# A decoder trunk in split fp32: the streamed activations take another place modulo 256 bytes, and stationary weight chunks are written 64 bytes further on

## The chip, the core and the metric

The kernel runs on one core of one Trainium2 chip. The metric is the device time of one execution in microseconds, and what is compared is the median of several runs. [...]

## What is computed

Two layers over 256 tokens of width 2048. Each layer is a mixing half and a feed-forward half, with a norm before and after each. Cut to what matters here:

```python
for l in range(DEPTH):                                  # DEPTH = 2
    hn = rms_norm(x, norm_mix_pre[l])
    proj = hn @ w_in[l]                                 # 2048 x 5888
    p_rwkv, p_attn, p_gmlp = jnp.split(proj, [...], axis=-1)
    y = concat(rwkv7_mix(p_rwkv), dilated_attention(p_attn), chunked_sgu(p_gmlp))
    x = x + rms_norm(y @ w_out[l], norm_mix_post[l])    # 2048 x 2048
    hn = rms_norm(x, norm_ffn_pre[l])
    up = hn @ ffn_up[l]                                 # 2048 x 11264
    conv = conv_b + causal_conv(up, width=3)
    gate, val = jnp.split(conv, 2, axis=-1)
    x = x + rms_norm((gelu(gate) * val) @ ffn_down[l], norm_ffn_post[l])   # 5632 x 2048
```

## The kernel before

Every large product is made in split form. A number is kept as a high part in fp32r, which TensorE takes as it is, and a low part, the rest. A product is then hi*hi + lo*hi + hi*lo, each of them a matmul in fp32r.

**Weights.** All large weights come through one stream of chunks, 128 partitions by 1024 numbers. SyncE's queue fetches a chunk into a tile raw (line 85), ScalarE casts it into whi (line 104), VectorE subtracts to make wlo (line 113). There are four buffers of whi and of wlo and three of raw (NB, RB = 4, 3). A few chunks at the seam between two halves go into other tiles instead (xw; xhi and xlo), for which extra holds a function. The list chunks names source and length of each chunk in the order of use; step() and wave_chunks() fill it.

**Activations.** act_tile() makes 16 tiles act of 512 numbers: 256 tokens of the high part, then 256 of the low part.

**Which operand is stationary.** TensorE holds one operand, 128 by 128, loaded by a weight load (PEld), and streams the other past it. The load for the next matmul runs while the present one streams.

- ws_step() (lines 528 and 529) holds the weights. For each of 16 blocks of the depth it streams all 512 numbers of act past whi, then the first 256 past wlo. It is used for the RWKV columns of w_in (output ps_r) and for ffn_up (ps_up).
- as_steps() (lines 554 to 556) holds the activations and streams the weights, 512 columns at a time (256 in one span and in a tail): high part past whi, high part past wlo, low part past whi. With act it is used for the other columns of w_in and for w_out; with hh and hl, the gated products of the feed-forward half, for ffn_down.
- Wave.part() (lines 315 to 318) is ws_step in 256 columns, for the first two outputs at the seam of two halves.

**Order.** Steps run in the order of the list steps, one chunk after another, and side work (the RWKV pairs, attention, the conv) is put between chunks by slot(), one piece of each generator at a time. The order of the instructions is thus that of the Python program; nothing is moved by a scheduler.

**Places.** The byte at which a tile starts in its partition follows from the order of allocation. In the built programs:

```text
tile                    start before  mod 256     start after  mod 256
act (16)                30976, ...       0        31200, ...     224
raw (3)                 184288, ...    224        182240, ...    224
whi, wlo (4 each)       196576, ...    224        194528, ...    224 (tile)
  written, stationary                  224                        32
  written, streamed                    224                       224
hh, hl (2 each)         94176, ...     224        94176, ...     224
xhi, xlo (3 each)       147424, ...    224        147424, ...    224
xw                                      32                         0
```

All blocks of 128 by 128 within these tiles begin a multiple of 512 bytes after the tile, so a block has the place of its tile.

Of the kernel before, what the change touches and what calls it, by code (L numbers as in the profile page):

```python
# [10 lines left out]
F32 = mybir.dt.float32  # L11
F32R = mybir.dt.float32r
# [8 lines left out]
P = 128  # L21
# [34 lines left out]
def tile_trunk(ctx, tc, x_d, xt_d, pos_d, cst_d, lvl_d, pcol_d, pcv_d, prow_d,  # L56
# [6 lines left out]
    const = ctx.enter_context(tc.tile_pool(name="const", bufs=1))  # L63
    wp = ctx.enter_context(tc.tile_pool(name="wp", bufs=NB, side="right"))
# [9 lines left out]
    chunks = []  # L74
# [5 lines left out]
    def emit_dma(upto=1 << 30):  # L80
        while st["dma"] < min(len(chunks), st["lo"] + RB, upto):
            w = st["dma"]
            src, n = chunks[w]
            raws[w] = wp.tile([P, 1024], F32, name="raw", bufs=RB)
            nc.sync.dma_start(raws[w][:, :n], src)
            st["dma"] += 1

    def emit_hi():
        w = st["hi"]
        if w == len(chunks):  # L90
            return
        if w in extra:
            pair = extra[w]()
            if pair is None:
                return
            hi, lo = pair
        elif sum(v not in extra for v in range(st["done"], w)) < NB:
            hi = wp.tile([P, 1024], F32R, name="whi")
            lo = wp.tile([P, 1024], F32R, name="wlo")
        else:  # L100
            return
        emit_dma()
        n = chunks[w][1]
        A.copy(hi[:, :n], raws[w][:, :n])  # L104
        whl[w] = (hi, lo)
        st["hi"] += 1

    def emit_lo():
        w = st["lo"]
        if w < st["hi"]:  # L110
            n = chunks[w][1]
            hi, lo = whl[w]
            V.tensor_tensor(lo[:, :n], raws.pop(w)[:, :n], f(hi[:, :n]), op=ALU.subtract)  # L113
            st["lo"] += 1
            emit_dma()

    def weight(ahead=0):
        while st["lo"] <= st["done"] + ahead:
            emit_hi()
            emit_lo()  # L120
        return whl[st["done"] + ahead]

    def mid():
        emit_hi()
        slot()

    def weight_done():
        del whl[st["done"]]
        st["done"] += 1
        emit_lo()  # L130
# [4 lines left out]
    def slot():  # L135
        for g in list(live):
            try:
                next(g)
            except StopIteration:
                live.remove(g)  # L140

    def boost():
        emit_hi()
        emit_lo()
# [2 lines left out]
        while live:  # L147
            slot()

    def step(srcs, fn):  # L150

        chunks.extend(srcs)
        steps.append(fn)


# [72 lines left out]
    def sumsq(src, acc, n, junk=None):  # L228
# [2 lines left out]
            junk = pmx.tile([P, 512], F32, name="junk", tag="mx")[:, :n]  # L231
        A.activation(junk, src, AF.Square, accum_out=acc)

    both = {}

    def act_tile():
# [20 lines left out]
    def big(n, name):  # L257
        return sm.tile([P, 2, ACOLS], F32, name=name, tag="big", bufs=1)[:, :, :n]
# [65 lines left out]
    def wave_chunks(tiles, post_in):  # L324
        if hasattr(post_in, "room"):
            for q in post_in.rooms:
                extra[len(chunks) + q] = lambda q=q: post_in.room(q)
        chunks.extend((t[0][:, h * 1024:(h + 1) * 1024], 1024) for h in range(2) for t in tiles)

    def rows_of(ss, wait=4, pool=None):  # L330

# [24 lines left out]
    def opening(gain0, act, tiles):  # L356
# [6 lines left out]
        q = xt.rearrange("p (c k) t -> p c (k t)", c=4)  # L363
        load(0)
        emit_dma(1)
        emit_dma(2)
        load(1)
# [150 lines left out]
    def ws_step(src, act, out, after):  # L518

        def fn():  # L520
            ps = out()
            for h in range(2):
                hi, lo = weight()
                for k in range(8):
                    kt = h * 8 + k
                    c = slice(k * P, (k + 1) * P)
                    ah, al = act[kt]
                    T.matmul(ps, hi[:, c], both[id(ah)][0], start=kt == 0, stop=False)  # L528
                    T.matmul(ps[:, S:], lo[:, c], ah, start=False, stop=kt == 15)  # L529
                    if k == 3:  # L530
                        mid()
                weight_done()
                if h == 0:
                    slot()
            after(ps)
            slot()
        step([(src[:, h * 1024:(h + 1) * 1024], 1024) for h in range(2)], fn)


    def as_steps(src, off, act, k0, nk, n, after, tail=0, more=False, late=0, hold=False):  # L540
# [67 lines left out]
    def add(items):  # L608
        for srcs, fn in items:
            step(srcs, fn)  # L610


    def mixing(l, post_in):
# [92 lines left out]
        def rw_tile(t, out, done=None):  # L706
            src, alloc, after = rw(t, out, done)
            ws_step(src, act, alloc, after)
# [516 lines left out]

        first = [rw(0, lambda: env["wa"], lora_w, pmx), rw(1, lambda: env["glo"], lora_g, pmx)]
        wave_chunks(first, post_in)
        steps.append(start)
        spans = [(0, 512), (512, 512), (1024, 512), (1536, 512), (2048, 256), (2304, 512), (2816, 512)]
# [84 lines left out]
        def evac1(n):  # L1314
            def after(i, ps):
                A.copy(env["yacc"][:, i, n * 512:(n + 1) * 512], ps)
            return after

        step([], pre1)
        step([], pre1b)  # L1320
        for n in range(4):
# [71 lines left out]
    def ffn(l, post_in):  # L1393
# [13 lines left out]
        def start():  # L1407
            boundary(l, "nffn", act, post_in(), first)
            fp = env["fp"] = es.enter_context(tc.tile_pool(name=f"fp{l}", bufs=1))
            env["pcv"] = fp.tile([P, NCV], F32, name="pcv")  # L1410
            nc.gpsimd.dma_start(env["pcv"], pcv_d[l])
            env["grow"] = fp.tile([P, D], F32, name="growf")
            nc.gpsimd.dma_start(env["grow"], bass.AP(tensor=prow_d.tensor,
                                                     offset=prow_d.offset + l * NPR + PR["nfp"],
                                                     ap=[[0, P], [1, D]]))
            fp.tile([P, 144], F32, name="gapf")
            env["yacc"] = big(D, "yaccf")
            env["ssq"] = sm.tile([P, 2, 5], F32, name="ssq", bufs=1)
            env["spare"] = lambda: fp.tile([P, 512], F32, name="yl", tag="pu", bufs=2)
# [53 lines left out]
        def up(g):  # L1473
            for q in range(1 if g == 0 else 0, GRP):
                for src, alloc, after in unit(g * GRP + q):
                    ws_step(src, act, alloc, after)
# [6 lines left out]

        first = [(wup[l, 0], alloc0, lambda ps: None), (wup[l, 1], alloc0, lambda ps: spawn(conv(0, pss)))]
        wave_chunks(first, post_in)
        steps.append(start)

        def down(g):
# [149 lines left out]
```

## Time and profile before

| | |
|---|---|
| median of 3 runs | 2491.04 us (2489.84 to 2491.28) |
| profiled execution | 2492.22 us |
| its span, first to last instruction | 2490.5 us |
| TensorE, matmuls | 98% of the span |
| VectorE, ScalarE, GpSimd | 71%, 54%, 22% |
| granted TensorE clock | 0.993 |
| DMA | 171 GB/s |

How to read it: the busy share of TensorE counts each matmul from its start to a modelled end, and matmuls overlap, so 98% does not say that it works at its peak. The rate is seen in the timeline of that engine, as the distance from one matmul's start to the next one's. [...]

The span runs through these stretches: 0 to 506 us the first layer's mixing half (RWKV pairs to 284), to 531 a seam, to 1248 its feed-forward half (up and down loops in turn), to 1267 a seam, to 1743 the second mixing half (RWKV pairs to 1520), to 1763 a seam, to the end the second feed-forward half.

### The profile page before, as it was taken

The page shows a single profiled execution, that of the slowest core. Times are in us where ns is not written, and L with a number is a line of the kernel's source. Part 1 is how long each engine was busy: PE and PEld are TensorE (multiplying, and loading weights), DVE is VectorE, ACT ScalarE, POOL GpSimd, SP SyncE. Part 2 cuts the span into 40 slices and gives each one's busy share as a digit, 9 for nine tenths or more (in the row PEclk, how much of TensorE's full clock was granted, in tenths as well). Part 3 has the DMA queues.
Part 4 walks back from the last instruction along what each step waited for, and adds up shares of the span by engine and source line. Part 5 has one row for each costly group of instructions (what it writes and reads, how often), then busy time and mean ns, then how long its engine had stood idle before and what let it go on. Part 6 is the DMA issues. An engine that isn't in the chain of part 4 may idle for free.

```text
span 2490.5 us, 37105 instructions
## 1 busy us (share of the span) xinstructions
PE 2432.9 (98%) x14010; PEld 2067.4 (83%) x14010; DVE 1760.1 (71%) x2584; ACT 1339.6 (54%) x2208; POOL 541.5 (22%) x512
## 2 busy tenths in 40 slices
PE   8999999999999999999999999999999999999998
PEld 7787787788888888888887877878888888888887
DVE  7889866577775675675678898665877756757755
ACT  5554545466555554554465555555665545545533
POOL 4224413031211120110232244132212101201102
PEclk9999999999999999999999999999999999999999
DMA  6343434645555555555543334345555565555554
GB/s 209 133 152 108 131 121 145 200 166 203 188 191 189 195 189 186 199 184 193 201 147 128 124 112 142 103 161 194 180 196 194 185 196 190 187 190 195 186 194 162
DMA packets 119762, 426.33 MB, mean 171 GB/s; under 512 B 13478, under 2 KB 13542, under 8 KB 119070
## 3 DMA queue, kind: packets, MB, share of 16 engines
q1 hardware_dynamic: 115776, 411.09, 49.0%
q0 software_dynamic: 2128, 9.59, 1.2%
q10 hardware_dynamic: 1678, 3.27, 0.5%
q8 instruction: 110, 1.80, 0.3%
q14 instruction: 70, 0.57, 0.1%
HBM read 421.80 MB, written 2.10 MB: 170 GB/s over the span
## 4 chain that ended last, share of the span: by engine, by line
PE 78%; DVE 7%; issue 6%; POOL 4%; ACT 3%; DMA 2%; DVEq 0%; POOLq 0%; ACTq 0%
PE ps_up L528 24%; PE ps_up L529 13%; PE ps_as L554 11%; PE ps_as L555 10%; PE ps_as L556 10%; PE ps_r L528 3%; DVE wlo L113 2%; PE ps_r L529 1%; DVE spl L821 1%; ACT whi L104 1%; POOL zv L1200 1%; DMA pcv<-in_pcv_dram 1%; POOL x L295 0%; DMA gws<-in_gws_dram 0%; ACT spl L830 0%
## 5 line engine op out<-in xcount | busy, mean ns | idle before, releaser
L113 DVE TENSOR_TENSOR wlo<-raw,whi 128x1024 fp32r<-128x1024 f32 (+1 forms) x785 | 975.4, 1250 | 385.6 <-ACT whi L104 383.7
L104 ACT CAST whi<-raw 128x1024 fp32r<-128x1024 f32 (+1 forms) x785 | 808.6, 1033 | 405.8 <-PE ps_as L556 168.7
L528 PE MATMUL ps_up<-act,whi 128*128 128x512 f32 x2752 | 954.7, 390 | 0.0
L529 PE MATMUL ps_up<-act,wlo 128*128 128x256 f32 x2752 | 776.2, 282 | 0.4 <-DVE wlo L113 0.3
L528 PEld LDWEIGHTS ps_up<-act,whi 128*128 128x128 f32 x2752 | 516.5, 188 | 108.1
L529 PEld LDWEIGHTS ps_up<-act,wlo 128*128 128x128 f32 x2752 | 520.1, 189 | 1.1 <-DVE wlo L113 1.0
L554 PE MATMUL ps_as<-whi,act 128*128 128x512 f32 (+1 forms) x712 | 289.5, 407 | 0.4 <-ACT act L253 0.4
L1457 POOL TENSOR_TENSOR cv<-cv,cv 128x256 f32<-128x256 f32 x88 | 70.6, 802 | 958.1 <-DVE cv L1452 958.1
L554 PE MATMUL ps_as<-whi,hh 128*128 128x512 f32 (+1 forms) x726 | 277.9, 383 | 0.0
L555 PE MATMUL ps_as<-wlo,hh 128*128 128x512 f32 (+1 forms) x726 | 277.8, 383 | 0.0
L556 PE MATMUL ps_as<-whi,hl 128*128 128x512 f32 (+1 forms) x726 | 277.7, 383 | 0.0
L556 PE MATMUL ps_as<-whi,act 128*128 128x512 f32 (+1 forms) x712 | 273.1, 384 | 0.0
L555 PE MATMUL ps_as<-wlo,act 128*128 128x512 f32 (+1 forms) x712 | 272.8, 383 | 0.0
L528 PE MATMUL ps_r<-act,whi 128*128 128x512 f32 x576 | 217.7, 412 | 0.0
L1435 ACT COPY pu<-ps_up 128x256 f32<-128x256 f32 x172 | 64.0, 372 | 255.8 <-PE ps_up L529 255.8
L529 PE MATMUL ps_r<-act,wlo 128*128 128x256 f32 x576 | 162.8, 283 | 0.0
L554 PEld LDWEIGHTS ps_as<-whi,hh 128*128 128x128 f32 x726 | 136.4, 188 | 26.9 <-DVE yaccf L1353 0.2
L556 PEld LDWEIGHTS ps_as<-whi,hl 128*128 128x128 f32 x726 | 136.4, 188 | 26.7
L555 PEld LDWEIGHTS ps_as<-wlo,hh 128*128 128x128 f32 x726 | 136.4, 188 | 26.5
L556 PEld LDWEIGHTS ps_as<-whi,act 128*128 128x128 f32 x712 | 134.1, 188 | 28.9 <-DVE act L254 0.4
L554 PEld LDWEIGHTS ps_as<-whi,act 128*128 128x128 f32 x712 | 134.7, 189 | 26.4 <-issue 4.0
L555 PEld LDWEIGHTS ps_as<-wlo,act 128*128 128x128 f32 x712 | 134.8, 189 | 21.9 <-DVE wlo L113 0.5
(380 smaller groups left out, 2950.2 us busy)
## 6 DMA issues: line engine op xcount, KB each, us to landing
raw<-in_wup_dram SPq DMA_DIRECT2D x352, 512.0 KB, 3.9
raw<-in_wdn_dram SPq DMA_DIRECT2D x160, 512.0 KB, 3.5
raw<-in_win_t_dram SPq DMA_DIRECT2D x104, 512.0 KB, 3.4
raw<-in_win_r_dram SPq DMA_DIRECT2D x80, 512.0 KB, 3.6
raw<-in_wo_dram SPq DMA_DIRECT2D x64, 512.0 KB, 3.6
raw<-in_wdn_dram SPq DMA_DIRECT2D x32, 256.0 KB, 2.7
xt<-in_xt_dram SPq DMA_DIRECT2D x4, 512.0 KB, 7.5
x<-in_x_dram ACTq DMA_DIRECT2D x4, 512.0 KB, 4.0
```

Of the source, the lines that this page charges most:

```text
L104: A.copy(hi[:, :n], raws[w][:, :n])
L113: V.tensor_tensor(lo[:, :n], raws.pop(w)[:, :n], f(hi[:, :n]), op=ALU.subtract)
L528: T.matmul(ps, hi[:, c], both[id(ah)][0], start=kt == 0, stop=False)
L529: T.matmul(ps[:, S:], lo[:, c], ah, start=False, stop=kt == 15)
L554: T.matmul(ps, ah[:, t], hi[:, c], start=kt == 0, stop=False)
L555: T.matmul(ps, ah[:, t], lo[:, c], start=False, stop=False)
L556: T.matmul(ps, al[:, t], hi[:, c], start=False, stop=kt == nk - 1)
L821: V.tensor_tensor(Sp[hs[1 - h], h], src[hs[h]], f(Sp[hs[h], h]), op=ALU.subtract)
L1200: G.tensor_tensor(vv[:, i], vv[:, i], rb_(nm), op=op)
L1435: A.copy(p[:, e], ps[e][:, S:])
L1457: G.tensor_tensor(cv[1], cv[0], cv[1], op=ALU.mult)
```

## The change

A gap of 224 bytes is allocated ahead of the act tiles, so that they start at place 224 modulo 256, as the weight tiles do. Another gap, in the feed-forward half, is made 224 bytes shorter, so that hh and hl stay where they were. Chunks get a third entry, whether they are held as the stationary operand; if so (ws_step and the waves), whi and wlo are written 16 numbers, 64 bytes, into their tile. The tiles grow from 1024 to 1088 numbers, 256 bytes, so that each of them starts at place 224 as before. Each engine carries out the same instructions in the same order on the same shapes; only addresses differ.

```diff
-            src, n = chunks[w]
+            src, n, _ = chunks[w]
...
-            hi = wp.tile([P, 1024], F32R, name="whi")
-            lo = wp.tile([P, 1024], F32R, name="wlo")
+            o = 16 * chunks[w][2]
+            hi, lo = (wp.tile([P, 1088], F32R, name=q)[:, o:o + 1024] for q in ("whi", "wlo"))
...
-    def step(srcs, fn):
-
-        chunks.extend(srcs)
+    def step(srcs, fn, still=False):
+
+        chunks.extend((*s, still) for s in srcs)
...
+    const.tile([P, 56], F32, name="gap")
     both = {}
 
     def act_tile():
...
-        chunks.extend((t[0][:, h * 1024:(h + 1) * 1024], 1024) for h in range(2) for t in tiles)
+        chunks.extend((t[0][:, h * 1024:(h + 1) * 1024], 1024, True) for h in range(2) for t in tiles)
...
-        step([(src[:, h * 1024:(h + 1) * 1024], 1024) for h in range(2)], fn)
+        step([(src[:, h * 1024:(h + 1) * 1024], 1024) for h in range(2)], fn, True)
...
-            fp.tile([P, 144], F32, name="gapf")
+            fp.tile([P, 88], F32, name="gapf")
```

## Rows read from the trace of the kernel before

**Rows 1.** The page: busy us and share by engine; clock in 40 slices.

```profile
PE 2432.9 (98%) x14010; PEld 2067.4 (83%) x14010; DVE 1760.1 (71%) x2584; ACT 1339.6 (54%) x2208; POOL 541.5 (22%) x512
...
PEclk9999999999999999999999999999999999999999
```

**Rows 2.** TensorE's waits: who waited for whom, us in total, times, longest.

```profile
PE ps_q L908 <- DVE X L919: 9.2, 12, 2.0
PE ps_t L437 <- DVE x L292: 6.9, 5, 3.0
PE ps_gm L1207 <- POOL zv L1200: 5.7, 2, 3.1
```

**Rows 3.** TensorE's timeline, as loop over act: start, us; first and last of 173.

```profile
439.70 0.40 PE L555 MATMUL ps_as<-wlo,act 128*128 128x512 f32 x1
...
479.83 0.40 PE L556 MATMUL ps_as<-whi,act 128*128 128x512 f32 x1
```

**Rows 4.** The same view, down loop over hh and hl: first and last of 178.

```profile
949.81 0.39 PE L556 MATMUL ps_as<-whi,hl 128*128 128x512 f32 x1
...
989.93 0.39 PE L556 MATMUL ps_as<-whi,hl 128*128 128x512 f32 x1
```

**Rows 5.** Instructions on single lines: ns min/median/max, first and last start.

```profile
L556 PE MATMUL ps_as<-whi,hl x726: 279/389/393, 764.5 to 2480.8; 128*128 128x512 f32 x171, 128*128 128x256 f32 x11
...
L556 PE MATMUL ps_as<-whi,act x712: 274/396/628, 48.8 to 1743.4; 128*128 128x512 f32 x158, 128*128 128x256 f32 x20
```

**Rows 6.** Windows of 46 us: TensorE busy (matmuls), clock, DMA share, GB/s; act, then hh.

```profile
435.00:481.00 46.00, 46.00 (x198) 1.00 0.60 195
...
950.00:996.00 46.00, 46.00 (x204) 1.00 0.58 191
```

**Rows 7.** Timeline of the up loop, weights stationary: first and last of 175.

```profile
2061.65 0.39 PE L528 MATMUL ps_up<-act,whi 128*128 128x512 f32 x1
2061.88 0.28 PE L529 MATMUL ps_up<-act,wlo 128*128 128x256 f32 x1
...
2091.81 0.39 PE L528 MATMUL ps_up<-act,whi 128*128 128x512 f32 x1
```

**Rows 8.** Timeline of the opening wave: eight matmuls of 256 columns, and the next.

```profile
21.22 1.09 PE L318 MATMUL ps_r<-act,whi 128*128 128x256 f32 x8
22.15 0.28 PE L315 MATMUL ps_r<-act,whi 128*128 128x256 f32 x1
```

**Rows 9.** TensorE's groups with shapes apart: count | busy us, mean ns | idle before.

```profile
L528 PE MATMUL ps_up<-act,whi 128*128 128x512 f32 x2752 | 954.7, 390 | 0.0
L529 PE MATMUL ps_up<-act,wlo 128*128 128x256 f32 x2752 | 776.2, 282 | 0.4 <-DVE wlo L113 0.3
L554 PE MATMUL ps_as<-whi,act 128*128 128x512 f32 x632 | 265.6, 420 | 0.4 <-ACT act L253 0.4
...
L528 PE MATMUL ps_r<-act,whi 128*128 128x512 f32 x576 | 217.7, 412 | 0.0
...
L555 PE MATMUL ps_as<-wlo,act 128*128 128x256 f32 x80 | 22.5, 281 | 0.0
L556 PE MATMUL ps_as<-whi,act 128*128 128x256 f32 x80 | 22.4, 280 | 0.0
```

**Rows 10.** Waits within 47:284 and 284:506; then windows: busy PE, PEld, DVE, ACT, POOL.

```profile
PE ps_q L908 <- DVE X L919: 5.2, 7, 1.9
...
PE ps_gm L1207 <- POOL zv L1200: 2.6, 1, 2.6
...
47.00:284.00 237.00, 226.44 (x1589) 184.93 (x1589) 204.25 (x392) 125.30 (x240) 74.25 (x78) 1.00 0.40 131
...
531.00:1248.00 717.00, 716.94 (x3840) 622.27 (x3839) 480.88 (x607) 390.24 (x564) 111.12 (x99) 1.00 0.57 194
```

**Rows 11.** The chunks' subtraction and cast into each kind of tile: ns min/median/max.

```profile
L113 DVE TENSOR_TENSOR wlo<-raw,whi x785: 682/1225/2605, 8.1 to 2471.0; 128x1024 fp32r<-128x1024 f32 x189, 128x512 fp32r<-128x512 f32 x8
...
L113 DVE TENSOR_TENSOR xw<-raw,xw x4: 1207/1210/1212, 506.0 to 1751.9; 128x1024 fp32r<-128x1024 f32 x4
...
L104 ACT CAST whi<-raw x785: 615/1052/1081, 7.0 to 2469.9; 128x1024 fp32r<-128x1024 f32 x189, 128x512 fp32r<-128x512 f32 x8
...
L104 ACT CAST xw<-raw x4: 1028/1042/1054, 502.9 to 1742.3; 128x1024 fp32r<-128x1024 f32 x4
```

**Rows 12.** Timeline of the second seam's wave, chunks of two places: first and last of 24.

```profile
527.09 0.28 PE L318 MATMUL ps_up<-act,whi 128*128 128x256 f32 x1
527.20 0.28 PE L318 MATMUL ps_up<-act,xw 128*128 128x256 f32 x1
...
529.80 0.28 PE L318 MATMUL ps_up<-act,xw 128*128 128x256 f32 x1
```

## What I expect, before the run

> **What bounds the kernel now.** I read the page's busy shares first: TensorE is busy 98% of the span, VectorE 71%, ScalarE 54%, at a granted clock of nine tenths or more in all 40 slices [rows 1]. Then the waits: the idle time ahead of TensorE, in 23 entries, comes to some 45 us in the whole span, the longest entry 9.2 us [rows 2]. So the end is set by how closely TensorE's matmuls follow one another, and the next view is the timeline of one engine, where the distance from start to start shows that.
>
> Three loops make nearly all of TensorE's time. The up loop (and the r loop of the mixing) has the weight chunk stationary and streams act, 512 columns for hi and 256 for lo. The two "as" loops stream the weights, 512 columns, past a stationary tile: act in the mixing, hh and hl in the down projection. The as loops issue the same instruction on the same shapes, from L554 to L556, yet differ. With act stationary, 172 intervals take from 439.70 to 479.83, which is 40.13 / 172 = 233.3 ns each; with hh and hl, 177 take from 949.81 to 989.93, which is 226.7 ns [rows 3, 4]. The durations agree: 396 against 389 ns, with no queue in between [rows 5]. In windows of the same 46 us 198 matmuls stand against 204, at the same granted clock of 1.00 and nearly the same DMA rate [rows 6].
>
> What else differs? The place of the operands in their partition, by the table of places ahead. I write d for the place modulo 256 of the tile whose weights are being loaded, less the place of the tile that streams meanwhile. With hh it is 224 - 224 = 0; with act it is 0 - 224, or +32. In the up and r loops it is 224 - 0, or -32. There a pair (512 and then 256 columns) takes from 2061.65 to 2091.81 for 87 pairs: 346.7 ns [rows 7].
>
> [...]
>
> **The change, part by part.**
>
> First, act moves from place 0 to place 224. For the as loops over act d becomes 0, as it is for hh. Of their matmuls 632 on each of the three lines have 512 columns [rows 9], so 1,896 intervals go from 233.3 to 226.7: 1,896 x 6.6 = 12.5 us less. The 240 with 256 columns I leave alone: at 280 to 281 ns on L555 and L556 they are no longer than the 282 ns of L529. Some of the gain is given back. In the as loops of the mixing other work runs between the chunks, and TensorE waits there 5.2 us for DVE X in the first pairs (seven waits) and 2.6 us for POOL zv [rows 10]; those chains keep their length while the matmuls that cover them get 3% shorter. I take 1.5 us for that, an estimate of about a tenth, and 11 us remain.
>
> Second, stationary weight chunks start 64 bytes on, at place 32, under act at 224: d in the up and r loops goes from -32 to +64. There are 2,752 + 576 = 3,328 pairs [rows 9], so each nanosecond of a pair is 3.3 us. No matmul of these loops has d = +64 in this trace, so I bound it by the nearest rows. [...] I take zero, and keep both ends for the range.
>
> Third, the chunks' cast and subtraction (L104, L113) write at place 32 from raw at 224, 64 bytes off, where both were at 224. The trace has just that pair of places: the xw tiles, at 32. Their cast takes 1042 ns against 1052 in the median, their subtraction 1210 against 1225 [rows 11]. This costs nothing.
>
> Fourth, the waves: 384 matmuls of 256 columns, whose loads go from -32 to +64, or to 0 for chunks in the tiles xhi and xlo, or stay at +32 (xw). At 4 ns each they are 1.5 us to either side, taken as zero. The rest is moved whole: tiles behind act go on by 224 bytes, hh and hl stay where they were because the second gap is 224 bytes shorter, and the ring of chunks grows downward into free space. No instruction is added, dropped or reordered, no DMA changes its size.
>
> The sum against the profiled execution, whose own time is 2492.2 us (span 2490.5 and 1.7 around it): 2492.2 - 11 = 2481 us. That execution lies 1.2 us over the median of the three runs, so against 2491.04 it is **2480 us**.
>
> [...]
>
> **The rivals.**
>
> The dear pair, which ends on the other side. At d = +64 a weight load meets the stream as it does at +32, since that is its nearest neighbour by address. It decides from a pair that is 11 / 3.3 = 3.3 ns dearer: there the two effects cancel. At 4.8 ns dearer the kernel is over 0.2% slower. [...] For it: the price is seen to rise from d = 0 to d = +32. Against it: in the mixed run of 256-column matmuls at +32 and -32, 23 intervals from 527.09 to 529.80 take 117.8 ns [rows 12], so +32 is not dear at every length.
>
> [...]
>
> Places are not the cause. The down loops run beside other work than the loops over act, and it may be that work, not the place, that makes 6.6 ns; reads of the stream and of the weights then don't meet at all. Then nothing moves: 2491 us. [...] Against it: clock and DMA rate are the same in the windows compared, and the excess is there in every interval.
>
> That the change doesn't do what it says is out: the built program has act at 224, the stationary chunks at 32, the streaming ones and hh at 224.
>
> **How the numbers follow.** The forecast, a pair within 1.6 ns of today's, lies between 2475 and 2486: chance 0.40. The cheap pair, below that: 0.26. The dear pair: from 1.6 to 4.8 ns it ends within 0.2% of before, 0.16; above that it is slower, 0.13. Places not the cause: 0.05, no change. Some 0.2%, or 5 us, is about what a measurement of this kernel can tell from no change. So faster 0.66, same 0.21, slower 0.13. The range goes from 2460 to 2497: it leaves out the last third of the cheap pair (about 0.07) and the upper part of the dear one (about 0.12).
>
> **What the profile after would show.** The as loops over act at 226.7 ns from start to start, 389 ns long, 204 matmuls in 46 us: the first term. [...] Down loops and the casts unchanged. If act's loops stay at 233, places are not the cause and the prediction is wrong at its root; if the pair moves by more than 2 ns, its second term is.

## The result: slower by 0.63%

The changed kernel takes 2508.15 us in the median of 6 runs (2504.57 to 2510.08), the kernel before 2492.38 (2489.84 to 2494.14, 6 runs). The ratio is 1.0063, with a 95% interval from 1.0053 to 1.0074. The forecast was 2480 us, and the range ended at 2497.

The profiled execution after the change has a span of 2508.4 us, 17.9 more than before. The granted clock is 0.992 of full speed, where it was 0.993. The page's first row, against [rows 1]:

```profile
PE 2446.5 (98%) x14010; PEld 2068.1 (82%) x14010; DVE 1762.0 (70%) x2584; ACT 1335.8 (53%) x2208; POOL 543.6 (22%) x512
```

TensorE's groups with shapes apart (lines behind the new gap are one higher: the loops are L529, L530 and L555 to L557); they answer to [rows 9]:

```profile
L529 PE MATMUL ps_up<-act,whi 128*128 128x512 f32 x2752 | 972.8, 397 | 0.0
L530 PE MATMUL ps_up<-act,wlo 128*128 128x256 f32 x2752 | 773.3, 281 | 0.0
...
L557 PE MATMUL ps_as<-whi,act 128*128 128x512 f32 x632 | 248.9, 394 | 0.0
L556 PE MATMUL ps_as<-wlo,act 128*128 128x512 f32 x632 | 247.7, 392 | 0.4 <-DVE wlo L113 0.4
```

The 512-column matmuls of the up loop last 397 ns where they lasted 390. Of the as loops over act, the second and the third matmul of a group last 392 and 394 ns; before they lasted 396 and 397:

```profile
L556 PE MATMUL ps_as<-whi,act 128*128 128x512 f32 x632 | 250.7, 397 | 0.0
L555 PE MATMUL ps_as<-wlo,act 128*128 128x512 f32 x632 | 250.3, 396 | 0.0
```

The windows of the two feed-forward halves tell where the time went (TensorE busy and matmuls first; the row of before is in [rows 10]):

```profile
530.00:1256.00 726.00, 726.00 (x3843) 622.03 (x3842) 480.22 (x607) 388.12 (x565) 113.01 (x99) 1.00 0.57 192
...
1772.00:2508.40 736.40, 726.93 (x3848) 622.72 (x3846) 485.10 (x614) 387.36 (x566) 116.36 (x101) 1.00 0.55 188
```

Each half takes 9 us more than before (726 against 717, 736.4 against 727.5). The timeline of TensorE in the second layer's up loop, first and last of 171 rows, as in [rows 7]:

```profile
2079.82 0.40 PE L529 MATMUL ps_up<-act,whi 128*128 128x512 f32 x1
2080.05 0.28 PE L530 MATMUL ps_up<-act,wlo 128*128 128x256 f32 x1
...
2109.85 0.40 PE L529 MATMUL ps_up<-act,whi 128*128 128x512 f32 x1
```

From 2079.82 to 2109.85 there are 85 pairs: 353.3 ns each, where it was 346.7. In 2,752 pairs 6.6 ns are 18.2 us, as much as the whole span grew. The as loop over act, first and last of 178 rows, against [rows 3]:

```profile
437.82 0.39 PE L556 MATMUL ps_as<-wlo,act 128*128 128x512 f32 x1
...
477.94 0.39 PE L556 MATMUL ps_as<-wlo,act 128*128 128x512 f32 x1
```

That is 40.12 / 177 = 226.7 ns, the value of the down loops: the first effect is there, and yet the two mixing halves together take no less time than before.

### The profile page after: what moved, and what is told of

It reads as the page before. It is cut to its first block, busy times and chain, and to the rows that moved or that the text cites. A ratio compares the mean times of both kernels' runs of the same rounds, so it can differ in the third digit from the quotient of the medians.

```text
span 2508.4 us, 37105 instructions
## 1 busy us (share of the span) xinstructions
PE 2446.5 (98%) x14010; PEld 2068.1 (82%) x14010; DVE 1762.0 (70%) x2584; ACT 1335.8 (53%) x2208; POOL 543.6 (22%) x512
## 4 chain that ended last, share of the span: by engine, by line
PE 81%; DVE 7%; issue 4%; POOL 3%; ACT 3%; DMA 1%; SPq 0%; DVEq 0%; ACTq 0%; POOLq 0%
PE ps_up L529 26%; PE ps_up L530 13%; PE ps_as L555 11%; PE ps_as L557 10%; PE ps_as L556 10%; PE ps_r L529 2%; DVE wlo L113 2%; PE ps_r L530 1%; DVE spl L822 1%; POOL zv L1201 1%; ACT whi L104 1%; DMA gws<-in_gws_dram 1%; PE ps_t L438 0%; ACT spl L831 0%; DVE x L293 0%
## 5 line engine op out<-in xcount | busy, mean ns | idle before, releaser
L529 PE MATMUL ps_up<-act,whi 128*128 128x512 f32 x2752 | 972.8, 397 | 0.0
L530 PE MATMUL ps_up<-act,wlo 128*128 128x256 f32 x2752 | 773.3, 281 | 0.0
L529 PEld LDWEIGHTS ps_up<-act,whi 128*128 128x128 f32 x2752 | 517.4, 188 | 127.5
L530 PEld LDWEIGHTS ps_up<-act,wlo 128*128 128x128 f32 x2752 | 516.6, 188 | 0.1
L555 PE MATMUL ps_as<-whi,act 128*128 128x512 f32 (+1 forms) x712 | 287.9, 404 | 0.4 <-ACT act L254 0.4
L555 PE MATMUL ps_as<-whi,hh 128*128 128x512 f32 (+1 forms) x726 | 278.0, 383 | 0.0
L557 PE MATMUL ps_as<-whi,hl 128*128 128x512 f32 (+1 forms) x726 | 277.8, 383 | 0.0
L557 PE MATMUL ps_as<-whi,act 128*128 128x512 f32 (+1 forms) x712 | 271.5, 381 | 0.0
L529 PE MATMUL ps_r<-act,whi 128*128 128x512 f32 x576 | 218.1, 413 | 0.0
L530 PE MATMUL ps_r<-act,wlo 128*128 128x256 f32 x576 | 162.1, 282 | 0.0
L555 PEld LDWEIGHTS ps_as<-whi,hh 128*128 128x128 f32 x726 | 136.4, 188 | 26.8
L557 PEld LDWEIGHTS ps_as<-whi,hl 128*128 128x128 f32 x726 | 136.4, 188 | 26.8
L557 PEld LDWEIGHTS ps_as<-whi,act 128*128 128x128 f32 x712 | 134.4, 189 | 26.7 <-DVE act L255 0.4
L555 PEld LDWEIGHTS ps_as<-whi,act 128*128 128x128 f32 x712 | 135.2, 190 | 24.4 <-issue 4.0
```

Of the source, the lines that this page charges most:

```text
L555: T.matmul(ps, ah[:, t], hi[:, c], start=kt == 0, stop=False)
L557: T.matmul(ps, al[:, t], hi[:, c], start=False, stop=kt == nk - 1)
```

## Experiments

All kernels below are the changed kernel with one line altered, `o = 16 * chunks[w][2]`, which says how many numbers of 4 bytes into its tile a chunk is written; where more was altered, the edit shows it. d is, as in the prediction, the place modulo 256 of the weights being loaded less that of the stream. Pairs and intervals are read from start to start in the timelines, over 85 to 87 pairs in the second of the three up stretches of layer two, unless it is said otherwise; the table's pairs are means over whole stretches. Each ratio is to runs of the kernel before on the same chip, so times of different groups are compared through it.

### One part alone, and the place of the stationary chunks

`e1_m32`: act moved, the up loop's d as before.

```diff
-            o = 16 * chunks[w][2]
+            o = 56 if chunks[w][2] else 0
```

> The change with one number altered: stationary chunks are written 224 bytes into their longer tiles instead of 64, so that in the up and r loops d, the place of the loaded weights less the place of the stream, is -32 as in the kernel before; act stays at 224, so d is 0 in the as loops. Theory A (the place alone sets a load's price): the up loop's pair goes back from 353.3 to 346.7 ns, the as loops over act keep 226.8 ns in uninterrupted stretches, and the time is some 5 to 11 us under the kernel before, 2482 to 2488 us. Theory B (something else in the change costs: the longer tiles, the moved ring of chunks, a cast that writes off the place of raw): the pair stays near 353 ns and the time near 2508 us.

2490.47 us against 2493.06, ratio 0.9991 (0.9982 to 1.0000). The pair is back. From the first to the last of 87 such rows:

```profile
2079.89 0.39 PE L529 MATMUL ps_up<-act,whi 128*128 128x512 f32 x1
...
2109.70 0.39 PE L529 MATMUL ps_up<-act,whi 128*128 128x512 f32 x1
```

In 29.81 us there are 86 pairs, 346.6 ns each. The tiles are as long and lie where they lie in the changed kernel, and the cast writes off the place of raw as well, so theory B falls: it is the place of the chunks. That the difference d counts, and not the two places by themselves, rests on one comparison: the kernel before has d = -32 with other places (act at 0, chunks at 224, where they are here at 224 and 192) and the same pair. And the first half of the change, now alone, brings 2.6 us, not 5 to 11.

`e2_zero`: act moved, chunks at the start of their tiles (`o = 0`).

> The move of act alone: stationary chunks are written at the start of their tiles, so d is 0 in the up and r loops as well as in the as loops. [...] Theory C (a load's price depends on the lengths that alternate as much as on d, so that the down loops say nothing of the pair): the pair differs from 346.8 by over 2 ns, and the time by over 7 us from theory A's.

2508.50 us, 1.0058 (1.0043 to 1.0073): as slow as the change. Theory A, by which the place alone sets the price, is out with its 2482 to 2488 us; theory C holds, and in an odd way. The first up stretch of a layer and the later ones differ, at the same places (first and last of 175 rows, then of 172, where the last L530 is left off):

```profile
599.72 0.39 PE L529 MATMUL ps_up<-act,whi 128*128 128x512 f32 x1
...
629.88 0.39 PE L529 MATMUL ps_up<-act,whi 128*128 128x512 f32 x1
```

```profile
2079.71 0.40 PE L529 MATMUL ps_up<-act,whi 128*128 128x512 f32 x1
...
2109.74 0.40 PE L529 MATMUL ps_up<-act,whi 128*128 128x512 f32 x1
```

The early one has 30.16 / 87 = 346.7 ns a pair, the later one 30.03 / 85 = 353.3. All of the first stretch has the one value, all of the two later ones the other, in both layers. The four dear stretches hold 1,404 pairs, 9.3 us. The rest of the loss, some 6 us of this execution, lies in the mixing halves (1.0 and 5.0 us), where TensorE's granted clock was lower: over the span it is 0.990, the lowest of all executions profiled here, against 0.993 before.

`e3_chunks_only`: the other half of the change alone, act at its old place.

```diff
+            o = 16 if chunks[w][2] else 0
...
-    const.tile([P, 56], F32, name="gap")
...
+            fp.tile([P, 144], F32, name="gapf")
```

> The other half alone: stationary chunks 64 bytes further on, act at its old place 0, so that d is +32 in the up and r loops, and +32 in the as loops over act as before. [...] Theory B (it is the tiles' length and place, not d): the pair is as after the change, 353.3 ns, and the time 2512 to 2516 us, as the as loops' gain is missing too. Theory C: the pair may lie anywhere from 340 to 355 ns.

2513.05 us, 1.0084 (1.0067 to 1.0101). The pair takes 353.3 ns in all stretches, 6.6 more than at -32; the time is what the dear pair and as loops at +32 make together. These are theory B's numbers, but its cause fell with `e1_m32`: the pair has the same value at +32 and at +64.

`e4_128`, `e5_m64`, `e6_m16`, `e7_96`, `f3_m96`: other places, act at 224, as loops at d = 0. The edit is `o = 32`, 48, 60, 24 and 40 for stationary chunks.

> Stationary chunks 128 bytes further on: d is +128 in the up and r loops, a place of which no run so far tells anything. Theory A gives no price beforehand: with that of -32 or 0 the time is 2482 to 2488 us, with that of +64 it is 2508 us. If a load is dear only in a stretch of places just above 0, the pair is 346.7 ns or less. Theory B: 2508 us, as the tiles are those of the change.

> Stationary chunks 192 bytes into their tiles, d = -64 in the up and r loops, act at 224. So far the up loop's pair took 346.8 ns at -32, 350.2 at 0, 353.3 at +32, 353.4 at +64, 351.1 at +128. Theory D (a smooth curve over 256 bytes with its low point between -128 and 0): -64 lies near the low point, the pair takes 345 to 348 ns, 2486 to 2494 us. Theory E (d = -32 is a narrow lucky place at which the two lengths lock into one rhythm): the pair is 349 to 352 ns, 2498 to 2508 us.

> Stationary chunks 240 bytes into their tiles, d = -16 in the up and r loops, half way between the places of two runs (346.8 ns a pair at -32, 350.2 at 0). Theory D: near the mean of both, 348 to 349 ns, 2494 to 2500 us. Theory E: as at 0 or worse, 350 ns and more, 2500 us and more. If places count in steps of 32 bytes, it is the same as one of its neighbours.

> Stationary chunks 96 bytes further on than the streaming ones by 96 bytes, d = +96 in the up and r loops. Theory D: between the pairs at +64 (353.4 ns) and +128 (351.1), 351 to 353 ns, 2503 to 2510 us. Theory E: no value beforehand, 349 to 354 ns.

> Up and r loops at d = -96, the as loops at 0. Theory D (a smooth curve) has no room left beside the pairs at -64 (351.1 ns), -32 (346.8), -16 (351.8) and +96 (346.7); a smooth one through the neighbours at 128 and -64 (both 351.1) gives 351 ns, 2504 us. Theory E gives anything from 346 to 354 ns. Theory F (modulo 128): -96 equals +32, 353.3 ns and 2508 us.

```text
d of the up loop   run              pair, ns (later stretches)   time, us   ratio (interval)
 -96               f3_m96           350.0                        2498.93    1.0028 (1.0017 to 1.0039)
 -64               e5_m64           348.9 (353.3 in the first)   2504.23    1.0038 (1.0024 to 1.0052)
 -32               e1_m32           346.7                        2490.47    0.9991 (0.9982 to 1.0000)
 -16               e6_m16           353.3 (once 346.7)           2504.86    1.0047 (1.0032 to 1.0062)
   0               e2_zero          353.3 (346.7 in the first)   2508.50    1.0058 (1.0043 to 1.0073)
 +32               e3_chunks_only   353.3                        2513.05    1.0084 (1.0067 to 1.0101)
 +64               the change       353.3                        2508.15    1.0063 (1.0053 to 1.0074)
 +96               e7_96            346.7                        2489.79    0.9987 (0.9977 to 0.9996)
+128               e4_128           351.1                        2503.02    1.0034 (1.0023 to 1.0046)
```

The loop of `e7_96`, first and last of 175 rows, has 30.16 / 87 = 346.7 ns:

```profile
2079.64 0.39 PE L529 MATMUL ps_up<-act,whi 128*128 128x512 f32 x1
...
2109.80 0.39 PE L529 MATMUL ps_up<-act,whi 128*128 128x512 f32 x1
```

The smooth curve of theory D is dead: +96 is cheap between two dear places, and -16 is as dear as 0 though it lies half way to the cheap -32. Theory F, places modulo 128, fits -32 and +96 but not -96 and +32. What is left is theory E, which named no single value beforehand and had none as low as 346.7 at +96: there are single values (346.7, 348.9, 350.0, 351.1, 353.3), each kept over hundreds of pairs. The kernel before stands at one of the two cheap places.

At -16 and -64, too, one place has two rates. The first stretch of a layer is 20 pairs, two small matmuls of other work (L345) and 652 pairs. At -64 the 20 pairs ran at 348.9 ns and the 652 behind the two small matmuls at 353.3, in both layers. At -16 it was 346.7 on both sides in layer one, and 346.7 ahead and 353.3 behind in layer two, past the same interruption (layer one, then layer two):

```profile
538.25 0.39 PE L345 MATMUL ps_b<-cst,rstd 128*128 128x128 f32 x2
538.40 0.48 PE L529 MATMUL ps_up<-act,whi 128*128 128x512 f32 x1
```

```profile
1774.96 0.39 PE L345 MATMUL ps_b<-cst,rstd 128*128 128x128 f32 x2
1775.11 0.48 PE L529 MATMUL ps_up<-act,whi 128*128 128x512 f32 x1
```

### The as loops at other places

`e8_all_m32`, `f1_as128`, `f2_as16`: the up loop at a cheap place, streaming chunks written into their tiles too.

```diff
-            o = 16 * chunks[w][2]
+            o = 56 if chunks[w][2] else 8
```

(24 and 32 for `f1_as128`, 24 and 60 for `f2_as16`.)

> d = -32 in every loop: stationary chunks at 224 bytes into their tiles, streaming chunks 32 bytes into theirs, so that the as loops over act and the down loops over hh have d = -32 too, where they had 0. Theory A (place alone): 512 columns at -32 took 228.4 ns within the up loop's pair, so both as loops go to 228.4 from 226.8 where uninterrupted; 3,900 such matmuls, some 4 to 6 us more than with as loops at 0 (2490.5 us), so 2494 to 2497 us. [...]

> Up and r loops at d = +96, the cheapest so far beside -32; streaming chunks 128 bytes into their tiles, so that the as loops over act and the down loops have d = 128 in place of 0. Theory E (a load is cheap only at single places where the loop locks into one rhythm): uninterrupted as loops leave 226.8 ns, 229 to 236, and the time is 8 to 36 us over the 2489.8 us of the run with d = +96 and 0. Theory F (the pair is cheap at -32 and at +96, so places count modulo 128): 226.8 ns again and 2490 us.

> Up and r loops at d = +96; the as loops and down loops at +16, half way between 0 (226.8 ns uninterrupted) and +32 (233.3). Theory D (a smooth curve): some 230 ns, 2495 to 2503 us. Theory E (narrow places): 231 to 236 ns, 2500 to 2515 us. If places count in steps of 32 bytes: 226.8 ns, 2490 us, or 233 ns.

2504.34, 2503.49 and 2514.24 us (1.0046, 1.0050 and 1.0092). The down loops of the three, first and last of 152, 131 and 129 rows:

```profile
954.61 0.40 PE L556 MATMUL ps_as<-wlo,hh 128*128 128x512 f32 x1
...
989.85 0.39 PE L557 MATMUL ps_as<-whi,hl 128*128 128x512 f32 x1
```

```profile
959.73 0.40 PE L555 MATMUL ps_as<-whi,hh 128*128 128x512 f32 x1
...
989.94 0.39 PE L556 MATMUL ps_as<-wlo,hh 128*128 128x512 f32 x1
```

```profile
959.71 0.40 PE L555 MATMUL ps_as<-whi,hh 128*128 128x512 f32 x1
...
990.00 0.40 PE L557 MATMUL ps_as<-whi,hl 128*128 128x512 f32 x1
```

These are 35.24 / 151 = 233.4 ns at d = -32, 30.21 / 130 = 232.4 at 128 and 30.29 / 128 = 236.6 at +16, against 226.7 at 0. At -32 the up loop has its cheapest pair, and the same place costs the as loops 6.7 ns a matmul: what is read off one loop does not hold for another whose lengths alternate differently. And 16 bytes from the cheap place lies the dearest one seen. At +16 the as loops over act, too, have two rates: the stretch of 204 matmuls takes 236.7 ns a matmul in layer one and 233.3 in layer two.

### The entry into the loop

`f4_entry`: `e2_zero` with two bf16 matmuls of 256 columns, which nobody needs, ahead of the second, third and fourth group of up steps in a layer. Two of these groups begin the later stretches; the other lies inside the first stretch, so that six pairs of matmuls are put in and not four.

```diff
+            o = 0 if chunks[w][2] else 0
...
         def up(g):
+            if g:
+                step([], lambda: keep_warm(1))
```

> As the run with d = 0 in all loops (2508.5 us), but with two short bf16 matmuls on TensorE ahead of each up stretch that follows a down loop; they take under half a microsecond each time and are wanted by nobody. In the run with d = 0 the first up stretch of each layer, entered after other work, took 346.7 ns a pair throughout, and the two later ones, entered straight from a down loop, 353.3 throughout, at the same places. Theory G (at one place two rhythms are stable, and how the loop is entered picks one): the later stretches can change over, to 346.7 ns or to another value; at 346.7 the time falls by 1,404 pairs x 6.6 ns = 9 us, less some 2 us for what is put in, to about 2500 us. Rival H (what runs beside the later stretches makes them dear): they stay at 353.3 ns and the time at 2508 to 2511 us.

2494.89 us, 1.0012 (0.9999 to 1.0025), against 1.0058 without them: work was added, and by the ratios some 11 us went. The timeline shows the entry, and the loop 25 us later:

```profile
2053.90 0.39 PE L557 MATMUL ps_as<-whi,hl 128*128 128x512 f32 x1
2054.13 0.39 PE L286 MATMUL ps_w<-warm 128*128 128x256 bf16 x2
2054.28 0.47 PE L529 MATMUL ps_up<-act,whi 128*128 128x512 f32 x1
```

```profile
2079.66 0.40 PE L529 MATMUL ps_up<-act,whi 128*128 128x512 f32 x1
...
2109.82 0.39 PE L529 MATMUL ps_up<-act,whi 128*128 128x512 f32 x1
```

87 pairs in 30.16 us are 346.7 ns; all six stretches of this execution have it. Rival H is out: beside the loop runs what ran before. At d = 0 two rhythms, distances that the loop keeps once it has them, are stable, and 0.15 us of other work at the entry decides for 350 pairs which one is kept. Not all of the gain is that: between the two profiled executions lie 16.4 us, of which 8.1 are in the feed-forward halves and 8.3 in the mixing halves, where both kernels do the same and the granted clock of `e2_zero` was lower (0.990 over the span against 0.993). The times of this kernel scatter from 2486.63 to 2501.71 us. The clock goes with a part of that, 0.997 in the shortest execution and 0.992 in the longest; but at 0.993 alone they run from 2491.13 to 2499.31. The kernel before, at the same 0.993, ran from 2490.98 to 2496.92. That other executions fall into the other rhythm in some stretches may explain the wider scatter, but only the profiled one was seen.

`g1_entry64`: the same matmuls in the changed kernel, and `g2_best`: `e7_96` once more, with more runs.

> The change as it is, d = +64 in the up and r loops, with two short bf16 matmuls on TensorE ahead of the four up stretches that follow a down loop. Theory G1 (place and entry together pick the rhythm, and +64 has a cheap rhythm too): some of the four stretches go to 346.7 ns, each 351 pairs x 6.6 ns = 2.3 us, up to 9 us off 2508, so 2499 to 2506 us. Theory G2 (at +64 the dear rhythm is the only stable one; 0 is special in that it has both): all stay at 353.3 ns and the time at 2507 to 2511 us.

> The run with d = +96 in the up and r loops and 0 in the as loops once more, in more rounds, as it stood lowest of all (2489.8 us, 0.9987 of the kernel before). Theory: the pair at 346.7 ns in all six up stretches as in the kernel before, the as loops over act at 226.7 where uninterrupted; 2 to 5 us under the kernel before, 2487 to 2491 us. If the gain was chance, the interval takes in 1.

`g1_entry64` takes 2509.68 us, 1.0067 (1.0052 to 1.0083). Its loop, first and last of 171 rows:

```profile
2079.76 0.40 PE L529 MATMUL ps_up<-act,whi 128*128 128x512 f32 x1
...
2109.79 0.40 PE L529 MATMUL ps_up<-act,whi 128*128 128x512 f32 x1
```

That is 30.03 / 85 = 353.3 ns, and all six stretches have it. So at +64 this entry finds no cheap rhythm; whether another would, was not tried. `g2_best` takes 2492.19 us, 0.9997 (0.9989 to 1.0006): with 346.7 ns in the up loop and 226.7 in the uninterrupted as loops it is no faster than the kernel before that can be measured. The same kernel had 0.9987 the first time, so whether it is faster by some tenth of a per cent stays open.

## Why the prediction was wrong, step by step

**What bounds the kernel: right.** The feed-forward halves took 717 and 727.5 us with 346.7 ns a pair, and 726 and 736.4 with 353.3. In the mixing halves the granted clock moved as well, which the prediction had left out: in the second one's last 223 us it was 0.99 before and 0.98 after.

**Places matter: right.** The same instructions, at other addresses alone, take 346.7 to 353.3 ns a pair and 226.7 to 236.7 a matmul. With the stream left in place and the stationary operand moved, the pair goes from 346.7 to 353.3 ns (before and `e3_chunks_only`) and a matmul of the as loops over act from 233.3 to 226.7 (before and after); the other way round, the pair of the later up stretches goes from 346.7 to 353.3 (before and `e2_zero`). Why the places count, no run shows.

**The first term, 11 us: right in direction, mis-sized.** It took 6.6 ns for each of 1,896 matmuls. That holds where they follow one another without a break: in the trace of before those are eight stretches with 876 matmuls, and from first to last start they take 203.6 us before and 199.4 after, 4.2 us less. Most of the others come in 160 pieces of six, between side work, which take 201.6 us before and 200.4 after. Before, and then after, the second to the sixth matmul of a piece:

```profile
338.07 0.40 PE L555 MATMUL ps_as<-wlo,act 128*128 128x512 f32 x1
...
339.00 0.39 PE L556 MATMUL ps_as<-whi,act 128*128 128x512 f32 x1
```

```profile
337.68 0.40 PE L556 MATMUL ps_as<-wlo,act 128*128 128x512 f32 x1
...
338.60 0.40 PE L557 MATMUL ps_as<-whi,act 128*128 128x512 f32 x1
```

Four intervals take 0.93 us before and 0.92 after. Averaged over all 173 pieces and stretches of the changed kernel, with intervals over 300 ns left out, the second to the fifth interval take 230.8, 233.0, 230.8 and 227.6 ns; from the eleventh on the mean is 226.7. The part given back, taken as 1.5 us, was too small. One wait of TensorE grew by 2.3 us (before, then after):

```profile
PE ps_t L247 <- DVE act L251: 1.0, 2, 0.6
```

```profile
PE ps_t L248 <- DVE act L252: 3.3, 2, 2.3
```

Behind the longer one, which ends at 1653.13 us, the granted clock fell. From 1655 to 1657 us it is 0.50, and the first matmuls of the as loop start 0.43 us apart; at the same work in the kernel before, 1642 to 1646 us, it is 1.00 with waits of 0.39 and 0.21 us.

```profile
1653.13 0.77 PE L248 MATMUL ps_t<-cst,sig 128*128 128x128 f32 x4 [2.32 <-DVE act L252]
...
1656.78 0.63 PE L556 MATMUL ps_as<-wlo,act 128*128 128x512 f32 x1
1657.21 0.63 PE L557 MATMUL ps_as<-whi,act 128*128 128x512 f32 x1
```

With a cheap pair the first half was worth 2.6, 3.3 and 0.6 us in three measurements, two of them of the same kernel.

**The second term, zero: this is the step that failed.** No run shows a term of zero: at d = +64 the up loop's pair took 353.3 ns in place of 346.7, 6.6 ns and 18 us more. The zero was the author's choice. It carries the pair of d = -32 [rows 7] over to another place, and the runs show that what a place costs depends on the loop as well: at -32 the up loop has its cheapest pair, 346.7 ns, and the as loops of `e8_all_m32` take 233.4, against 226.7 at 0. The other choice in the trace of before was the difference of its two as loops, 233.3 against 226.7 ns a matmul [rows 3, 4]: 6.6 ns in each of 3,328 pairs are 22 us, an estimate from these rows. The r loops' 576 pairs add next to nothing to that: 116 of their pieces are four pairs long, and those take 377 ns a pair before and 375 after. Their 512-column matmuls last 413 ns in the mean, against 412 in [rows 9]:

```profile
L529 PE MATMUL ps_r<-act,whi 128*128 128x512 f32 x576 | 218.1, 413 | 0.0
```

So of the 28 us between forecast and result 18 are this term; 1.3 are the median of before, which came out higher with more runs, and the other 9 or so fit the first term, which was worth 0.6 to 3.3 us in place of 11. The dear rival named the place and the direction, and its slower part was given 0.13. Its ground, that +64 acts as +32, was right: at +32 the pair takes 353.3 ns as well. That the pair lost the same 6.6 ns by which the two as loops differ is in part luck: `e8_all_m32` shows that a price of these loops (6.7 ns more at -32 than at 0) need not hold in the up loop, which has its cheapest pair at -32. Its evidence against, that 256-column matmuls at +32 were not dear, came from a loop of another alternation as well.

The waves were taken as zero beside 4 ns a matmul, an estimate of the author's that no run shows. In the opening one eight matmuls take 0.93 us before [rows 8] and 0.91 after, at d = +64:

```profile
20.88 1.07 PE L319 MATMUL ps_r<-act,whi 128*128 128x256 f32 x8
21.79 0.28 PE L316 MATMUL ps_r<-act,whi 128*128 128x256 f32 x1
```

**The casts off raw's place: right.** Their medians are 1054 and 1225 ns, against 1052 and 1225 in [rows 11].

**The range.** Its lower end, 2460 us, was kept for a cheaper pair; that was the author's estimate, and no run shows a pair under 346.6 ns. Its upper end, 2497 us, left out the upper part of the dear rival, and let every rival keep the full 11 us of the first term; even with all of the 22 us, 2491 - 11 + 22 = 2502 us, it lies under the result. Bounds of both terms together, no gain and 22 us, would have reached 2491 + 22 = 2513 us and held it.

## What to carry to other kernels

In this kernel the cost that comes with the places of the two operands is a rhythm of the loop, not a price per instruction (at d = 0 the up loop has 346.7 or 353.3 ns a pair): a row tells it only for the loop, the alternation of lengths, the addresses and the entry at which it was read. Before such a place is moved for one loop, look at which other loop shares the tile, and take both bounds for it. And a gain per instruction that is read in long stretches is to be counted over long stretches only: here these held 876 of 1,896 matmuls.

## What the runs showed of the hardware

- One loop at fixed addresses has two stable rates: 346.7 and 353.3 ns a pair at d = 0. Each was kept over stretches of 352 or 652 pairs, and two matmuls of 0.15 us together at the entry moved the loop from one to the other. The same was seen at -16 (346.7 and 353.3), at -64 (348.9 and 353.3) and in the as loops at +16 (233.3 and 236.7 ns a matmul).
- At d = -32 and +96 all six up stretches of the profiled executions had the cheap rate, 346.7 ns, at +32 and +64 all six the dear one, 353.3. Why these places, is open; so is whether some entry other than the one tried would change +64. That places repeat after 256 bytes was assumed and not tested.
- Work that nobody needs went with a shorter time of this kernel: 1.0012 of the time before with it (`f4_entry`), 1.0058 without (`e2_zero`).
- A wait of 2.32 us on TensorE was followed by a granted clock of 0.50, and matmuls of 512 columns 427 ns apart in place of 227.
